# Seven products for two k-tile pairs in the first two down products of both FFNs, with the sums of their rows made behind the last up group

## The chip, the cores and the metric

The kernel runs on one core of one Trainium2 chip. The metric is the device time of one execution in microseconds; the time before is the median of three runs. The engines go by their short names: PE (TensorE, matmuls), PEld (its weight loads), DVE (VectorE), ACT (ScalarE), POOL (GpSimd) and SP (SyncE, which issues the DMAs here).

## The reference

One layer of a streaming encoder on 256 rows of 2048 features, all in fp32:

```python
def swiglu(h, w_gate, w_up, w_down):
    return (jax.nn.silu(h @ w_gate) * (h @ w_up)) @ w_down
...
x = x + 0.5 * swiglu(rms_norm(x, ffn1_norm[l]), ffn1_w_gate[l], ffn1_w_up[l], ffn1_w_down[l])
...
x = x + 0.5 * swiglu(rms_norm(x, ffn2_norm[l]), ffn2_w_gate[l], ffn2_w_up[l], ffn2_w_down[l])
return rms_norm(x, final_norm)
```

Between the two FFNs stand a pooling and gated-linear-attention mixer and a cross attention over 256 memory tokens, which the change does not touch. The FFN's width (D_FF) is 5632: gate and up weights are 2048 x 5632, down weights 5632 x 2048. The profile shows 418 MB read from HBM.

## The kernel before

**Products.** An fp32 value is kept as a high part (rounded to the fp32r form) and a low part (the rest), and a product is three matmuls: high x high, high x low, low x high (`products`). Rows of activations lie transposed in `xs` (the FFN's input) and `ys` (gate times up, or the other blocks' outputs) as 16 k tiles of 128 features by 256 rows, each in two parts. A row half is 128 rows.

**Units.** The stream (`Stream`) cuts all weights into units of 1 MB: two k tiles by 1024 columns in most of the FFN. For each unit SP loads a raw tile (three buffers), ACT copies it into the high part `wh`, DVE subtracts to the low part `wl` (`split_weights`, three buffers each), two units ahead of the matmuls. `in_turn` keeps these copies in the order of the units on each engine. A plain unit is 24 matmuls of 128x128 by 512 columns: two column halves j, two k tiles, two row halves, three matmuls each (`block_t`).

**Seven products.** In a unit whose number in its block is 0, 2 or 4 (`PAIRS`) of the gate and up blocks, the two k tiles and two row halves are taken as a 2 x 2 block matrix, and the unit makes seven products in place of eight (`seven`, 21 matmuls). This needs sums of weight blocks (`add_weights`, tile T on DVE, then a high and low part of T and of three of the raw blocks, xh and xl, in `split_seven`), and sums of row blocks (`part_sums`, made once per FFN and kept in `xe`). The products gather in seven PSUM banks; after the last seven unit `combine` reads four of them (ACT copies one, DVE adds), and at the block's end `join` brings in the rest, once per column half j (`block_s`). The down products of before have no sevens: they are `block_t`, a plain sum in two PSUM tiles.

**PSUM.** Four tiles of two banks, all eight banks. `block_s` holds all four from its first seven unit until `combine`, `block_t` holds two. The turn below takes two for a moment.

**The FFN.** 5632 columns are 11 blocks of 512, worked in parts of 4, 4 and 3 (`FF_PARTS`). The first two parts each are: a gate and an up block of 1024 columns (8 units each), a second gate and up block, then the down product of this part's 16 k tiles (`into_x`): two column halves b of 1024 columns, 8 units each. So a part is 32 units of gate and up and 16 of down; the text calls the four blocks of 8 the first to fourth block of a part. After each up block the product gate x up (`ev_up`) is turned by sixteen transposes on PE in two PSUM tiles `ph` (`turn`), and split into `ys`. The turn of the last up block is queued one unit into the down product. The down product is added to x (`residual`, after `fetch_x` has loaded the columns of x) and written back (`store_x`).

**What sets the order.** `st.op(f, after)` queues a step so many units later; apart from that and from `in_turn`, a scheduler orders each engine's instructions once, at build time, by its own model of their times. On the chip each engine runs its list in that order, and waits where an operand is late. So an instruction that waits holds up everything behind it on its engine. SP's and ACT's and DVE's lists are all made so.

The lines that matter here: L228 and L229 (copy and low part of a weight), L234 and L235 (those of activations), L307 (matmul in `products`), L401 (matmul in `seven`), L363 to L367 (T), L443 to L448 (`combine`), L452 (`join`), L608 (`residual`), L681 (`ev_up`), L691 (transposes of `turn`).

Of the kernel before, what the change touches and what calls it, by code (L numbers as in the profile page):

```python
# [14 lines left out]
P = 128  # L15
# [77 lines left out]
def build(ctx, tc, I, out):  # L93
# [132 lines left out]

    def split_weights(hi, lo, src):
        in_turn("scalar", lambda: nc.scalar.copy(hi, src))  # L228
        in_turn("vector", lambda: nc.vector.tensor_tensor(  # L229
            out=lo, in0=src, in1=f32(hi), op=ALU.subtract  # L230
        ))
# [109 lines left out]
    def part_sums(act, ext, i, g):  # L341

        t = scope["pool"].tile([P, 4 * NB], F32, tag="T", name=uid("T"))
        a = t[:, :NB].rearrange("p (k s) -> p k s", k=2)
        e = t[:, NB : 2 * NB].rearrange("p (n s) -> p n s", n=4)
        nc.vector.tensor_tensor(
            out=a, in0=f32(act[:, 2 * g : 2 * g + 2, 0, :]), in1=f32(act[:, 2 * g : 2 * g + 2, 1, :]),
            op=ALU.add,
        )
        a11, a21, a12, a22 = (a[:, k, h * P : (h + 1) * P] for k in range(2) for h in range(2))  # L350
        nc.vector.tensor_tensor(out=e[:, 3], in0=a11, in1=a21, op=ALU.subtract)
        nc.vector.tensor_tensor(out=e[:, 1], in0=a22, in1=a21, op=ALU.subtract)
        nc.vector.scalar_tensor_tensor(
            out=e[:, 2], in0=e[:, 1], scalar=-1.0, in1=a11, op0=ALU.mult, op1=ALU.subtract
        )
        nc.vector.tensor_tensor(out=e[:, 0], in0=a12, in1=e[:, 2], op=ALU.add)
        split(ext[:, i, 0], ext[:, i, 1], e)
# [27 lines left out]
    def seven(banks, act, ext, i, g, first, later, weights):  # L385
# [3 lines left out]
        n4, n1, s2, s3 = ([ext[:, i, p, n] for p in range(2)] for n in range(4))  # L389
# [6 lines left out]
        order = ("P1", "P7", "P5", "P6", "P2", "P3", "P4") if first else (  # L396
            "P1", "P2", "P3", "P7", "P5", "P6", "P4")
        for n in order:
            (a, b), wh, wl = table[n]
            for j, (x, w) in enumerate(((a, wh), (a, wl), (b, wh))):  # L400
                nc.tensor.matmul(  # L401
                    banks[n], x, w, start=first and j == 0,
                    stop=not later and n in ("P1", "P5", "P6", "P7") and j == 2,
                )

    def block_s(srcs, act, ext, pairs, evict, delays=(0, 0)):

        held, n = {}, len(srcs)

        def open_banks():  # L410
            a, b, c, d = (ptile(uid("pt")) for _ in range(4))
            held["ps"] = (d, c)
            held["parts"] = (a, b)
            held["banks"] = {
                "P1": a[:, 0], "P6": a[:, 1], "P7": b[:, 0], "P5": b[:, 1],
                "P2": c[:, 0], "P4": c[:, 1], "P3": d[:, 0],
            }

        def unit_s(g):
            def fn(weights):  # L420
                if g == pairs[0]:
                    open_banks()
                seven(held["banks"], act, ext, pairs.index(g), g, g == pairs[0], g != pairs[-1],
                      weights)
            return fn

        def unit_p(g):
            def fn(wh, wl):
                wh, wl = (w.rearrange("p (k j n) -> p k j n", j=2, n=NB) for w in (wh, wl))
                for j in (1, 0):  # L430
                    for h in range(2):
                        for kk in range(2):

                            fresh = (j, h) == (0, 1) and g == min(set(range(n)) - set(pairs)) and kk == 0
                            products(held["ps"][j][:, h, :], act, 2 * g + kk, h, wh[:, kk, j],
                                     wl[:, kk, j], fresh, g == n - 1 and kk == 1)
            return fn

        def combine():
# [164 lines left out]
    def residual(scale, b):  # L604

        def evict(j, ps):
# [4 lines left out]
            if j:  # L611
                store_x(b)
        return evict

    def fold(c, gain):
# [10 lines left out]
        for h in range(2):  # L626
            q = tmp.tile([P, NB], F32, tag="j", name=uid("j"), bufs=2)
            nc.scalar.activation(q, x[:, h], AF.Square, accum_out=ss[:, h, c : c + 1])

    def into_x(w, act, scale, gain=None, k0=0, nk=KT, spread_too=True, src=None):  # L630
# [14 lines left out]
    PAIRS = (0, 2, 4)  # L645

    def pair_sums(g, delay):
        def f():
            if g == PAIRS[0]:
                rows["xe"] = scope["pool"].tile(  # L650
                    [P, len(PAIRS), 2, 4, P], F32R, tag="xe", name=uid("xe")
                )
            part_sums(xs, rows["xe"], PAIRS.index(g), g)
        st.op(f, delay)

    class Ext:


        def __getitem__(self, i):
# [650 lines left out]
```

## Time and profile before

| | |
|---|---|
| median of 3 runs | 2132.9 us (2132.69 to 2133.01) |
| the profiled execution | 2133.11 us, span 2131.2 us, mean granted clock 0.999 |
| PE busy | 2111.3 us, 99% of the span, 10032 matmuls and transposes |
| weight loads of PE (PEld) | 1768.5 us, 83% |
| DVE busy | 1427.7 us, 67%, 1189 instructions |
| ACT busy | 1008.0 us, 47%, 890 instructions |
| DMA | 204 GB/s over the span, queue q1 60.5% of 16 engines |

The profile is one execution on the chip. A line such as `L229 DVE TENSOR_TENSOR wl<-T,wh 128x2048 ... x54 | 123.6, 2288 | ...` is a group: its line in the kernel, engine, operation, output and inputs, size, count, busy us in all and mean ns of one, then the idle time of the engine before them and what ended it. A row of waits gives engine and line, what it waited for, us in total, times, and the longest. A row of the chain gives start, us and what ran (`x106`: so many instructions in one piece).

### The profile page before, as it was taken

The numbers are of one execution on the slowest core, as the hardware profiler recorded it, in microseconds if no ns is written. First come the engines' busy times: TensorE is split into PE (matmuls) and PEld (weight loads), VectorE is DVE, ScalarE is ACT, GpSimd is POOL, SyncE is SP. The second block draws the span as 40 slices with busy tenths as digits, with TensorE's granted clock in tenths as the row PEclk, the third lists the DMA queues.
The fourth block names the chain that finished last, engine by engine and source line by source line (L and its number), as shares of the span: only waits on it lengthen the run. The fifth ranks groups of instructions, "written<-read, shape, count | busy, mean of one in ns | idle before, by whom it ended". The sixth has DMA issues, their size and how long they took to land.

```text
span 2131.2 us, 24070 instructions
## 1 busy us (share of the span) xinstructions
PE 2111.3 (99%) x10032; PEld 1768.5 (83%) x10032; DVE 1427.7 (67%) x1189; ACT 1008.0 (47%) x890; POOL 14.2 (1%) x41
## 2 busy tenths in 40 slices
PE   9999999999999999999999999999999999999998
PEld 7878888888888888888888888888888888888886
DVE  8876588856864576565666454567874888658744
ACT  7554354534534545455445443445443455434433
POOL 0000000000000000000000000000000000000001
PEclk9999999999999999999999999999999999999999
DMA  7556665566656655557654555666576665766663
GB/s 277 197 189 234 224 221 195 186 233 226 227 178 234 221 162 180 167 185 278 222 190 161 167 169 171 195 207 207 175 247 217 214 209 175 249 212 223 221 217 119
DMA packets 143316, 435.91 MB, mean 205 GB/s; under 512 B 9828, under 2 KB 13000, under 8 KB 142824
## 3 DMA queue, kind: packets, MB, share of 16 engines
q1 hardware_dynamic: 143176, 434.38, 60.5%
q8 instruction: 78, 1.28, 0.2%
q14 instruction: 30, 0.25, 0.0%
q10 hardware_dynamic: 32, 0.01, 0.0%
HBM read 417.58 MB, written 16.78 MB: 204 GB/s over the span
## 4 chain that ended last, share of the span: by engine, by line
PE 98%; DVE 1%; issue 0%; ACT 0%; DMA 0%; SPq 0%; DVEq 0%; ACTq 0%
PE pt L307 58%; PE pa L292 15%; PE pt L401 12%; PE pb L307 6%; PE pe L307 3%; PE ph L691 1%; PE pl L1084 1%; PE pv L1119 1%; PE px L621 0%; DVE wl L229 0%; ACT wh L228 0%; DMA x<-in_x 0%; PE px L575 0%; PE po L954 0%; PE pa L832 0%
## 5 line engine op out<-in xcount | busy, mean ns | idle before, releaser
L229 DVE TENSOR_TENSOR wl<-raw,wh 128x2048 fp32r<-128x2048 f32 (+2 forms) x328 | 740.2, 2258 | 544.5 <-ACT wh L228 543.9
L228 ACT CAST wh<-raw 128x2048 fp32r<-128x2048 f32 (+2 forms) x328 | 618.5, 1886 | 721.7 <-PE pt L307 490.5
L307 PE MATMUL pt<-wh,xs 128*128 128x512 f32 x1952 | 618.6, 390 | 0.0
L307 PE MATMUL pt<-wh,ys 128*128 128x512 f32 x1728 | 534.7, 389 | 0.0
L307 PEld LDWEIGHTS pt<-wh,xs 128*128 128x128 f32 x1952 | 366.6, 188 | 75.7
L307 PE MATMUL pt<-wl,xs 128*128 128x512 f32 x976 | 380.8, 390 | 0.0
L307 PEld LDWEIGHTS pt<-wh,ys 128*128 128x128 f32 x1728 | 324.1, 188 | 67.0
L307 PE MATMUL pt<-wl,ys 128*128 128x512 f32 x864 | 336.3, 389 | 0.0
L292 PE MATMUL pa<-xs,wh 128*128 128x512 f32 x896 | 317.1, 398 | 2.1 <-DVE t L266 1.7
L292 PE MATMUL pa<-xs,wl 128*128 128x256 f32 x896 | 248.8, 281 | 0.0
L307 PEld LDWEIGHTS pt<-wl,xs 128*128 128x128 f32 x976 | 183.5, 188 | 37.9
L292 PEld LDWEIGHTS pa<-xs,wh 128*128 128x128 f32 x896 | 167.7, 188 | 41.2 <-issue 2.0
L307 PEld LDWEIGHTS pt<-wl,ys 128*128 128x128 f32 x864 | 162.2, 188 | 33.5
L292 PEld LDWEIGHTS pa<-xs,wl 128*128 128x128 f32 x896 | 169.2, 189 | 1.6 <-issue 0.2
L228 ACT CAST wh<-T 128x2048 fp32r<-128x2048 f32 x54 | 103.3, 1912 | 135.6 <-DVE T L367 93.3
L229 DVE TENSOR_TENSOR wl<-T,wh 128x2048 fp32r<-128x2048 f32 x54 | 123.6, 2288 | 65.3 <-ACT wh L228 65.3
L307 PE MATMUL pb<-wh,xs 128*128 128x512 f32 x384 | 121.7, 392 | 0.5 <-DVE ys L211 0.5
L401 PE MATMUL pt<-wh,xe 128*128 128x512 f32 x324 | 108.7, 389 | 0.0
L229 DVE TENSOR_TENSOR xl<-raw,xh 128x1536 fp32r<-128x1536 f32 x54 | 94.5, 1750 | 2.7 <-ACT xh L228 2.7
L228 ACT CAST xh<-raw 128x1536 fp32r<-128x1536 f32 x54 | 79.9, 1479 | 28.9 <-PE pt L401 28.8
L307 PEld LDWEIGHTS pb<-wh,xs 128*128 128x128 f32 x384 | 72.0, 188 | 15.6 <-DVE ys L211 0.7
L401 PE MATMUL pt<-xh,xs 128*128 128x512 f32 x216 | 78.6, 389 | 1.7 <-DVE sg L452 1.7
(203 smaller groups left out, 1666.3 us busy)
## 6 DMA issues: line engine op xcount, KB each, us to landing
raw<-in_ffn_w_down SPq DMA_DIRECT2D x88, 1024.0 KB, 5.5
raw<-in_ffn_w_up SPq DMA_DIRECT2D x80, 1024.0 KB, 5.0
raw<-in_ffn_w_gate SPq DMA_DIRECT2D x77, 1024.0 KB, 5.0
raw<-in_w_in SPq DMA_DIRECT2D x32, 1024.0 KB, 5.2
raw<-in_xattn_w_kv SPq DMA_DIRECT2D x32, 1024.0 KB, 5.2
raw<-in_w_out SPq DMA_DIRECT2D x16, 1024.0 KB, 6.2
raw<-in_xattn_w_q SPq DMA_DIRECT2D x16, 1024.0 KB, 5.2
raw<-in_xattn_w_o SPq DMA_DIRECT2D x16, 1024.0 KB, 5.6
```

The costliest lines, as they stand in the source:

```text
L228: in_turn("scalar", lambda: nc.scalar.copy(hi, src))
L229: in_turn("vector", lambda: nc.vector.tensor_tensor(out=lo, in0=src, in1=f32(hi), op=ALU.subtract))
L292: nc.tensor.matmul(o, w, x, start=k == 0 and i == 0, stop=last and i == 1)
L307: nc.tensor.matmul(ps, a, w, start=first and i == 0, stop=last and i == 2)
L401: nc.tensor.matmul(banks[n], x, w, start=first and j == 0, stop=not later and n in ("P1", "P5", "P6", "P7") and j == 2,)
L691: nc.tensor.transpose(v[:, i, h * P : (h + 1) * P], g[:, h, i * P : (i + 1) * P], ident)
L1084: nc.tensor.matmul(ps[:, t, :M], ys[:, 4 * h + d, a, tok], xa["K"][:, d, b, :], start=i == 0, stop=i == 11,)
L1119: nc.tensor.matmul(ps[:, d, :S], xa["V"][:, m, a, col], xa["PT"][:, m, b, :], start=i == 0, stop=i == 5,)
```

## The change

In the down products of the first two parts of both FFNs, the units of k-tile pairs 0 and 2 (`Y_PAIRS`) become seven units, and the eight pairs of a block are taken in the order 1, 3, 0, 4, 2, 5, 6, 7 (`Y_ORDER`). `block_s` is generalised for this: plain units may come ahead of the first seven unit, the PSUM tiles are opened when first needed, and the eighth bank (P0) takes the plain products. With `merge` given, the block's `combine` is followed right away by two additions of its four sums into x (`early_parts`), and the two joins at the end become plain residual additions; x is written back after column half 0 rather than 1. The sums of rows of `ys` (`y_sums`, tile `ye`) are made during the last up block, four and five units after that block is queued, put behind the latest low part and copy of a weight (`behind_weights`); one of the four sums is written over the row half it replaces in `ys`. The sums of `xs` are made the same way (in a `j` tile rather than in T) and queued 5, 6 and 7 units in, in both FFNs (before: 5, 5, 5 in the first, 3, 4, 5 in the second). The tile `j` has one buffer in place of two.

```diff
--- before.py
+++ after.py
         else:
             latest[engine] = f()
 
+    def behind_weights(f):
+        with tc.issue_after(latest["vector"].ins), tc.issue_after(latest["scalar"].ins):
+            f()
     def split_weights(hi, lo, src):
         in_turn("scalar", lambda: nc.scalar.copy(hi, src))
         in_turn("vector", lambda: nc.vector.tensor_tensor(
     def row_squares(src, c):
 
         for h in range(2):
-            j = tmp.tile([P, S], F32, tag="j", name=uid("j"), bufs=2)
+            j = tmp.tile([P, S], F32, tag="j", name=uid("j"))
             nc.scalar.activation(j, src[h], AF.Square, accum_out=ss[:, h, c : c + 1])
 
     diag, rows = {}, {}
 
 
 
...
+    def jtile():
+        return tmp.tile([P, NB], F32, tag="j", name=uid("j"))
+    class Sums:
+        def __init__(self, name, act, pairs, over):
+            self.name, self.act, self.pairs, self.over = name, act, pairs, over
+        def make(self, g):
+            act, i = self.act, self.pairs.index(g)
+            n = 3 if self.over else 4
+            if i == 0:
+                self.tile = scope["pool"].tile(
+                    [P, len(self.pairs), 2, n, P], F32R, tag=self.name, name=uid(self.name)
+                )
+            a, k = jtile(), slice(2 * g, 2 * g + 2)
+            nc.vector.tensor_tensor(
+                out=a.rearrange("p (k s) -> p k s", k=2), in0=f32(act[:, k, 0, :]),
+                in1=f32(act[:, k, 1, :]), op=ALU.add,
+            )
+            a = a.rearrange("p (n s) -> p n s", n=4)
+            p11, p21, p12, p22 = (a[:, m] for m in range(4))
+            nc.vector.tensor_tensor(out=p11, in0=p11, in1=p21, op=ALU.subtract)
+            nc.vector.tensor_tensor(out=p21, in0=p22, in1=p21, op=ALU.subtract)
+            nc.vector.scalar_tensor_tensor(
+                out=p22, in0=p11, scalar=-1.0, in1=p22, op0=ALU.mult, op1=ALU.subtract
+            )
+            nc.vector.tensor_tensor(out=p12, in0=p12, in1=p22, op=ALU.add)
+            split(self.tile[:, i, 0], self.tile[:, i, 1], a[:, 4 - n :])
+            if self.over:
+                split(act[:, 2 * g, 0, P:], act[:, 2 * g, 1, P:], p11)
+        def parts(self, g):
+            i, n = self.pairs.index(g), 3 if self.over else 4
+            t = [[self.tile[:, i, p, m] for p in range(2)] for m in range(n)]
+            return [[self.act[:, 2 * g, p, P:] for p in range(2)]] + t if self.over else t
 
     def add_weights(u, raw):
         t = scope["pool"].tile([P, 4 * NB], F32, tag="T", name=f"T{u}")
 
         return [parts], None
 
-    def seven(banks, act, ext, i, g, first, later, weights):
+    def seven(banks, act, sums, g, fresh, ends, weights):
         th, tl, rh, rl = weights
         k0, k1, lo, hi = 2 * g, 2 * g + 1, slice(0, P), slice(P, S)
         a11, a12, a22 = ([act[:, k, p, t] for p in range(2)] for k, t in ((k0, lo), (k1, lo), (k1, hi)))
-        n4, n1, s2, s3 = ([ext[:, i, p, n] for p in range(2)] for n in range(4))
+        s3, n1, n4, s2 = sums.parts(g)
         table = {
             "P1": (a11, rh[:, 0], rl[:, 0]), "P3": (n4, rh[:, 1], rl[:, 1]),
             "P2": (a12, rh[:, 2], rl[:, 2]), "P5": (n1, th[:, 0], tl[:, 0]),
             "P7": (s3, th[:, 1], tl[:, 1]), "P6": (s2, th[:, 2], tl[:, 2]),
             "P4": (a22, th[:, 3], tl[:, 3]),
         }
-        order = ("P1", "P7", "P5", "P6", "P2", "P3", "P4") if first else (
+        order = ("P1", "P7", "P5", "P6", "P2", "P3", "P4") if "P1" in fresh else (
             "P1", "P2", "P3", "P7", "P5", "P6", "P4")
         for n in order:
             (a, b), wh, wl = table[n]
             for j, (x, w) in enumerate(((a, wh), (a, wl), (b, wh))):
                 nc.tensor.matmul(
-                    banks[n], x, w, start=first and j == 0,
-                    stop=not later and n in ("P1", "P5", "P6", "P7") and j == 2,
-                )
-
...
+    def block_s(srcs, act, sums, order, evict, merge=None):
+        sevens = [g for g in order if g in sums.pairs]
+        held, seen = {"banks": {}}, set()
+        def banks(*names):
+            t = ptile(uid("pt"))
+            for i, n in enumerate(names):
+                held["banks"][n] = t[:, i]
+            return t
+        def open_whole():
+            if "ps" not in held:
+                c = banks("P2", "P4")
+                held["ps"] = (banks("P3", "P0"), c)
+        def open_parts():
+            held["parts"] = (banks("P1", "P6"), banks("P7", "P5"))
+        names = {(1, 0): "P2", (1, 1): "P4", (0, 0): "P3", (0, 1): "P0"}
 
         def unit_s(g):
             def fn(weights):
...
+                if g == sevens[0]:
+                    open_parts()
+                open_whole()
+                fresh = {f"P{i}" for i in range(1, 8)} - seen
+                seen.update(fresh)
+                ends = ("P1", "P5", "P6", "P7") if g == sevens[-1] else ()
+                seven(held["banks"], act, sums, g, fresh, ends, weights)
             return fn
 
         def unit_p(g):
             def fn(wh, wl):
+                open_whole()
                 wh, wl = (w.rearrange("p (k j n) -> p k j n", j=2, n=NB) for w in (wh, wl))
                 for j in (1, 0):
                     for h in range(2):
+                        n = names[j, h]
                         for kk in range(2):
-
-                            fresh = (j, h) == (0, 1) and g == min(set(range(n)) - set(pairs)) and kk == 0
-                            products(held["ps"][j][:, h, :], act, 2 * g + kk, h, wh[:, kk, j],
-                                     wl[:, kk, j], fresh, g == n - 1 and kk == 1)
+                            products(held["banks"][n], act, 2 * g + kk, h, wh[:, kk, j],
+                                     wl[:, kk, j], n not in seen and kk == 0,
+                                     g == order[-1] and kk == 1)
+                        seen.add(n)
             return fn
 
         def combine():
                 out=e[:, 1:3], in0=b, in1=e[:, 3:4].to_broadcast([P, 2, NB]), op=ALU.add
             )
             nc.vector.tensor_tensor(out=e[:, 3], in0=b[:, 1], in1=e[:, 1], op=ALU.add)
+            if merge is not None:
+                merge(e[:, 2:4], e[:, 0:2])
 
         def join(j):
+            if merge is not None:
+                evict(j, held["ps"][j])
+                return
             e = held["e"][:, 0:2] if j else held["e"][:, 2:4]
             nc.vector.tensor_tensor(
                 out=e, in0=held["ps"][j], in1=e, op=ALU.add if j else ALU.subtract
             )
             evict(j, e)
 
-        for g, src in enumerate(srcs):
-            if g in pairs:
-                st.unit(src, unit_s(g), split_seven, add_weights)
-                if g == pairs[-1]:
+        for g in order:
+            if g in sevens:
+                st.unit(srcs[g], unit_s(g), split_seven, add_weights)
+                if g == sevens[-1]:
                     st.op(combine)
             else:
-                st.unit(src, unit_p(g))
+                st.unit(srcs[g], unit_p(g))
         for j in (1, 0):
-            st.op(lambda j=j: join(j), delays[j])
+            st.op(lambda j=j: join(j))
 
     def block_b(srcs, act, evict, delay=0):
 
         for h in range(2):
             nc.sync.dma_start(X[b][h * P : (h + 1) * P, :], xrows[b][:, h])
 
-    def residual(scale, b):
+    def residual(scale, b, last=1):
 
         def evict(j, ps):
             x = x_cols((2 * b + j) * NB, NB)
             nc.vector.scalar_tensor_tensor(
                 out=x, in0=ps, scalar=scale, in1=x, op0=ALU.mult, op1=ALU.add
             )
-            if j:
+            if j == last:
                 store_x(b)
         return evict
+    def early_parts(scale, b):
+        def merge(minus, plus):
+            for j, e, s in ((1, plus, scale), (0, minus, -scale)):
+                x = x_cols((2 * b + j) * NB, NB)
+                nc.vector.scalar_tensor_tensor(
+                    out=x, in0=e, scalar=s, in1=x, op0=ALU.mult, op1=ALU.add
+                )
+        return merge
 
     def fold(c, gain):
 
...
+    def into_x(w, act, scale, gain=None, k0=0, nk=KT, spread_too=True, src=None,
+               sums=None):
 
         for b in range(2):
             st.op(lambda b=b: fetch_x(b, src), 2)
-            block_t(wwide(w, b * 2 * NB, k0, nk), act, residual(scale, b))
+            cols = wwide(w, b * 2 * NB, k0, nk)
+            if sums is None:
+                block_t(cols, act, residual(scale, b))
+            else:
+                block_s(cols, act, sums, Y_ORDER, residual(scale, b, 0), early_parts(scale, b))
             if gain is not None:
                 for j in range(2):
                     st.op(lambda c=2 * b + j: fold(c, gain), 1)
 
     FF_PARTS = ((0, 4), (4, 4), (8, 3))
 
-    PAIRS = (0, 2, 4)
-
...
+    PAIRS, Y_PAIRS = (0, 2, 4), (0, 2)
+    Y_ORDER = (1, 3, 0, 4, 2, 5, 6, 7)
+    CLEAR = PAIRS[-1] + 2
 
     def ffn(wg, wu, wd, down):
         gate = {}
+        x_sums = Sums("xe", xs, PAIRS, False)
+        y_sums = Sums("ye", ys, Y_PAIRS, True)
 
         def hidden():
             e = scope["pool"].tile([P, 4, NB], F32, tag="sg", name=uid("sg"), bufs=2)
                     )
             split(ys[:, k : k + 4, 0, :], ys[:, k : k + 4, 1, :], v)
 
+        for i, g in enumerate(PAIRS):
+            st.op(lambda g=g: x_sums.make(g), 5 + i)
         for lo, n in FF_PARTS:
+            whole = n == KT // 4
             for b in range(0, n - 1, 2):
                 n0 = (lo + b) * NB
                 if lo == b == 0:
                     block_t(wwide(wg, n0), xs, lambda j, ps: ev_gate(j, ps, 1))
                 else:
-                    block_s(wwide(wg, n0), xs, Ext(), PAIRS, lambda j, c: ev_gate(j, c, 0))
-                block_s(wwide(wu, n0), xs, Ext(), PAIRS, ev_up)
+                    block_s(wwide(wg, n0), xs, x_sums, range(8), lambda j, c: ev_gate(j, c, 0))
+                if whole and b:
+                    for i, g in enumerate(Y_PAIRS):
+                        st.op(lambda g=g: behind_weights(lambda: y_sums.make(g)), CLEAR - 2 + i)
+                block_s(wwide(wu, n0), xs, x_sums, range(8), ev_up)
                 held = {}
                 st.op(lambda held=held: held.update(gate))
-                wait = PAIRS[-1] + 2 if b + 2 < n - 1 else 1
+                wait = CLEAR if b + 2 < n - 1 else 1
                 for j in range(2):
                     st.op(lambda j=j, b=b, held=held: turn(held[j], 4 * (b + j)), wait)
             if n % 2:
...
+            down(wd, 4 * lo, 4 * n, lo + n == FF // NB, y_sums if whole else None)
 
     st.op(lambda: turn_gains(0, G_MIX))
     for c in range(8):
...
-    for g in PAIRS:
-        pair_sums(g, 5)
+    def down_first(wd, k0, nk, last, sums):
+        into_x(wd, ys, 0.5, G_MIX if last else None, k0, nk, src=None if k0 else I["x"][0],
+               sums=sums)
     ffn(I["ffn1_w_gate"][0], I["ffn1_w_up"][0], I["ffn1_w_down"][0], down_first)
     st.op(close_scope, 1)
     st.op(open_scope("s_mix"), 1)
...
```

More of the change, by code (lines that the diff above doesn't have):

```diff
@@ L401, in seven @@
                 nc.tensor.matmul(
[L402 to L417 removed]
+                    banks[n], x, w, start=n in fresh and j == 0, stop=n in ends and j == 2
+                )
+    def block_s(srcs, act, sums, order, evict, merge=None):
[13 more added lines that the diff above has]
+        names = {(1, 0): "P2", (1, 1): "P4", (0, 0): "P3", (0, 1): "P0"}
         def unit_s(g):
             def fn(weights):
[L421 to L424, printed above, removed]
+                if g == sevens[0]:
[5 more added lines that the diff above has]
+                seven(held["banks"], act, sums, g, fresh, ends, weights)
             return fn
```

40 lines of the change are left out of this document (4 added, 36 removed).

## The prediction

> **What bounds the kernel now.** I read the page first (busy shares, the chain that ended last), then what the matmul engine waits for, then the chain and the timelines around a down product and inside a part.
>
> ```profile
> PE 2111.3 (99%) x10032; PEld 1768.5 (83%) x10032; DVE 1427.7 (67%) x1189; ACT 1008.0 (47%) x890; POOL 14.2 (1%) x41
> ...
> PE 98%; DVE 1%; issue 0%; ACT 0%; DMA 0%; SPq 0%; DVEq 0%; ACTq 0%
> ```
>
> PE is the bound: 98% of the chain. A matmul taken off it is time gained, unless PE waits instead. The waits of PE, longest first:
>
> ```profile
> PE pgain L539 <- DMA gain<-in_ffn_norm: 4.1, 1, 4.1
> PE pt L401 <- DVE sg L452: 1.7, 1, 1.7
> PE pa L292 <- DVE t L266: 1.7, 1, 1.7
> PE po L954 <- DVE ST L947: 1.0, 1, 1.0
> ```
>
> All of them make some 10 us of 2131.2. The second is the kind that matters here: a seven-product unit waits because VectorE was at a join. The chain of waits around the second part's first down product, and VectorE's and ScalarE's timelines there:
>
> ```profile
> 421.07 2.04 PE pt L401 x9
> 423.11 24.03 PE pt L307 x106
> 447.14 1.75 PE ph L691 x16
> 448.89 1.15 PE pt L307 x5
> ```
>
> ```profile
> 448.27 1.93 ACT L234 CAST ys<-ph 128x1024 fp32r<-128x1024 f32 x2 [1.68 <-PE ph L691]
> ```
>
> ```profile
> 449.32 2.35 DVE L235 TENSOR_TENSOR ys<-ph,ys 128x1024 fp32r<-128x1024 f32 x2 [0.40 <-ACT ys L234]
> ```
>
> 106 matmuls in 24.03 us are 0.2267 us each. The sixteen transposes (L691) end at 448.89; ScalarE's copies end at 450.20 and VectorE's lows at 451.67, and PE runs straight on, because nothing it does in those 2.8 us reads the turned rows. Load by stretch (the columns after the span are PE, PEld, DVE, ACT, POOL, clock, DMA share, GB/s): the two down halves of the first part, then three of the second part's four gate and up blocks:
>
> ```profile
> 182.00:226.60 44.60, 44.60 (x206) 37.16 (x205) 24.89 (x16) 17.24 (x10) 0.00 (x0) 1.00 0.67 236
> 226.60:271.40 44.80, 44.80 (x199) 37.08 (x199) 28.72 (x19) 18.07 (x10) 0.00 (x0) 1.00 0.61 211
> 271.40:312.40 41.00, 41.00 (x183) 33.95 (x182) 33.95 (x26) 20.15 (x12) 0.00 (x0) 1.00 0.67 231
> 312.40:353.50 41.10, 41.10 (x183) 34.04 (x182) 34.66 (x26) 22.61 (x16) 0.00 (x0) 1.00 0.60 205
> 353.50:397.00 43.50, 43.50 (x202) 36.16 (x201) 37.21 (x30) 22.17 (x15) 0.00 (x0) 1.00 0.58 194
> ```
>
> VectorE has 16 to 20 us free in a down block, 6 to 7 in a block with sevens. So the change spends PE time for VectorE time where there is room, and the question is order, not sum.
>
> **What it removes.** 2 FFNs x 2 parts x 2 column halves x 2 pairs = 16 units go from 24 matmuls to 21: 48 x 0.2267 = 10.88 us off PE. The chain's own pieces agree: 5.44 us for 24 (L307), 4.76 for 21 (L401). DMA is the same: the same weight tiles are loaded. [...]
>
> **What it adds, off PE.** Per seven unit VectorE builds T (1.22 + 0.69 + 0.69) and xl (1.75), ScalarE xh (1.48); per block one combine (ACT 0.59; DVE 0.69 + 1.22 + 0.69) and two merges of 128x1024 at the residual's 1.22. Two sevens, combine and merges make 2 x 4.35 + 2.6 + 2.44 = 13.7 us of VectorE in a down block, against 16 to 20 free: hidden by sum. The row sums (Sums.make over ys) are 0.69, four 128x128 operations of 0.28, a low part of 0.28 and one of about 0.5, so some 2.6 us, twice per part, in the last up block, on top of 32.2 of 41.7 us in that stretch; the copies on ScalarE (47% busy) are short. They stand behind a weight's low part, so the low parts after them come up to 1.4 us later each; the weights are two units ahead there. I cost them at nothing (bounds 0 and 2 x 1.4 per part, 11 in all). Without that cover each microsecond is one of PE. The x sums move from 5, 5, 5 (and 3, 4, 5) to 5, 6, 7 units: three times about 2.5 us of VectorE at each FFN's start, where the weights of the first gate block need no T: nothing. One j buffer for two makes ScalarE's squares wait for each other (0.41 us each), while ScalarE is half idle: nothing. On SP's queue only the order of x loads and stores against weight loads changes; fetch_x of the second half stands behind the merges of the first, 20 us before its use: nothing.
>
> **What it moves, 1: the turn before the down product (four places).** In the new PE order the sixteen transposes come 56 matmuls after the down product starts (37 before), and behind them stand one matmul, then four of pair 4's unit, which read the just-turned rows: first the high parts (ScalarE's copy), at the third matmul the low parts (VectorE's). Then six matmuls open a bank pair that the turn must free. Before, plain units 1 to 3 lay between. From the rows: the first ph's copy can start 0.26 us after its transposes (448.27 against the eighth transpose), takes 1.015, the low part 1.22, and 0.1 to PE: 0.26 + 1.015 + 0.03 + 1.22 + 0.1 = 2.62 us. Cover: 0.65 (the rest of the other ph's transposes) and three matmuls, 0.68. PE waits 1.3 us, at four places 5.2. Bounds: 0.8 if VectorE's low part is not needed at once (ScalarE's copy alone), 2.6 if VectorE is a weight's low part (2.29) late at half the places: 3 to 8 in all.
>
> **What it moves, 2: the join in the second part.** VectorE leaves the second down half with its merges, about 4.5 us later than before (the walk of its queue by the rows above gives the low part of the second part's fourth unit 13.1 us after the part begins; in the trace it is 8.6). The first two blocks have 1.6 to 2.6 us of slack for that. At the third block's start the new VectorE order is: join of the block before, then wl of its first unit, two gate products, wl, the other join, xl, T of the next seven. Before, both T and that wl stood ahead of the first join:
>
> ```profile
> 309.54 2.29 DVE L229 TENSOR_TENSOR wl<-raw,wh 128x2048 fp32r<-128x2048 f32 x1 [0.63 <-ACT wh L228]
> 311.75 0.68 DVE L367 TENSOR_TENSOR T<-T,raw 128x512 f32<-128x512 f32 x1
> 312.35 1.22 DVE L452 TENSOR_TENSOR sg<-pt,sg 128x1024 f32<-128x1024 f32 x1
> 313.49 1.75 DVE L229 TENSOR_TENSOR xl<-raw,xh 128x1536 fp32r<-128x1536 f32 x1
> ```
>
> That timeline is of the second block's start, where T already stands right ahead of the join. With the join first, the first wl ends 0.26 + 1.22 + 2.29 + 0.1 = 3.87 us after PE is half through the last unit; PE wants it after 2.72 + 0.91 = 3.63: a wait of 0.25. T of the third unit then ends near 14.3 us, its copy on ScalarE at 16.2, its low part at 18.5, and PE, which interleaves units 2 and 3 there, asks for copies and low part at about 15.2 and 17.4: waits of 0.9 and 1.1. With 0.35 further on and 1.05 at the last up block's second seven: 3.65 us. In the second FFN the third block has the same order (2.6); the fourth has another one, where I take half of the 1.05. Together 3.65 + 3.1 = 6.75, bounds 0 (each wait is within 1.2 us of none) and 15.75 (below).
>
> **Sum.** -10.88 + 5.2 + 6.75 = +1.1 us on the profiled execution's 2133.11 us, which is 0.2 above the median of 2132.9: 2134.0 us.
>
> **Rivals.** Of the measurement, 0.2% (4.3 us) is about what can be told from no change.
>
> *Only the turn waits (the late copies of the second part vanish).* For: each is about a microsecond, VectorE is 83% busy there, and the turn waits give it time to catch up. Against: the join's place is an order, not a lag. 2132.9 - 10.88 + 5.2 = 2127.2.
>
> *Both are hidden.* For: the kernel before has the same interleaving in the third block with no wait. Against: the transposes' readers follow at once by the order. 2122.0.
>
> *VectorE becomes the bound in the second part (slower).* The wait of 2.25 us at the third block recurs at the second and fourth, in both FFNs: four times more, 9 us: 2134.0 + 9 = 2143. It decides from 2137.2 on, so from 3.2 us of waits beyond my sum: if two of the four come. For: 37.2 of 43.5 us busy even before, and the 1.7 us at the join in the first part. Against: the window still has 6 us.
>
> *PE's clock falls after the new waits.* One unit at half the clock after each turn wait would cost 4 x 5.44 = 21.8 us: 2156. Rows of the profile speak against it (after the span: PE busy and its count, clock, DMA share, GB/s): after the 1.7 us wait at 139 us the granted clock stayed at full:
>
> ```profile
> 139.00:141.00 2.00, 0.30 (x2) 1.00 0.96 381
> 141.00:143.00 2.00, 2.00 (x9) 1.00 0.08 33
> ```
>
> [...]
>
> That the products are not saved is no rival: the program has 48 matmuls fewer.
>
> **How the numbers follow.** Forecast 0.36 (2129 to 2138, its waits bounded as above); turn waits only 0.25; all hidden 0.12; VectorE the bound 0.25; the clock 0.02. Faster 0.25 + 0.12 = 0.37, same 0.36, slower 0.25 + 0.02 = 0.27. The range, 2122 to 2143, leaves out half of the all-hidden case and the upper part of the bound case, some 0.17.
>
> **What would show it.** PE: 48 matmuls fewer, 70 units of 21 for 54. Among PE's waits: four near 1.3 us on ys, by ScalarE or VectorE, right after the turn's transposes (near 195, 452 and twice in the second FFN), each over 0.8; waits on wh, wl or sg at the third block of both second parts, about 1 us each. VectorE's busy time: 16 x 4.35 (T and xl) + 8 x 2.6 (combines) + 8 x 2.44 (merges) + 8 x 2.6 (sums) = 131 us more, so 1558 us or 73% of the span. I am wrong if PE has none of these waits (2122), if only the first kind is there (2127), or if the second kind stands at every block's start of the second parts (2143).

## The result and the profile after

| | before | after |
|---|---|---|
| median | 2133.01 us (2132.63 to 2135.11, 9 runs) | 2138.74 us (2137.09 to 2139.99, 9 runs) |
| ratio | | 1.0022, 95% interval 1.0013 to 1.0031 |
| profiled execution (span) | 2133.11 us (2131.2) | 2139.99 us (2138.2) |
| matmuls and transposes on PE | 10032 | 9984 |
| DVE busy | 1427.7 us | 1541.1 us |

The 48 matmuls are gone, VectorE has 113 us more to do, and the kernel is slower: the saved 10.9 us were spent on waiting, and some 5 us more. The page of the changed kernel, in the two lines that were shown of before (busy time; then the chain that ended last, by engine):

```profile
PE 2109.6 (99%) x9984; PEld 1760.6 (82%) x9984; DVE 1541.1 (72%) x1349; ACT 1040.5 (49%) x930; POOL 15.3 (1%) x41
...
PE 91%; DVE 6%; issue 1%; ACT 1%; DMA 0%; SPq 0%; DVEq 0%; ACTq 0%
```

The busy share of PE hides it (99% in both); the chain shows it: PE carries 91% of it instead of 98%, and VectorE 6%. What PE waits for in the changed kernel (us in total, times, longest; the waits that before has too are left out but for the one at the join, which was 1.7 us once):

```profile
PE pt L312 <- ACT ys L239: 2.8, 4, 0.9
PE pt L429 <- DVE sg L499: 2.5, 3, 1.7
PE pt L429 <- DVE xl L234: 2.1, 2, 1.3
PE pt L312 <- ACT wh L233: 1.7, 2, 0.8
...
PE pt L429 <- ACT wh L233: 1.2, 2, 0.6
```

The first row is the turn, four times, once per down product with sevens. The others are in the second part of each FFN, but for the longest on `sg` (1.7 us), which is before's wait at 139 us in the first part. (Lines have moved: L312 is `products`, L429 `seven`, L499 `join`, L391 to L395 T, L733 `ev_up`, L743 the transposes, L233 and L234 a weight's copy and low part.)

**The turn.** The chain at the second part's first down product, which ran 447.14, 448.89 and straight on before:

```profile
454.86 1.54 PE ph L743 x14
456.40 0.02 issue
456.43 1.02 ACT ys L239
457.45 0.02 issue
457.47 1.24 DVE ys L240
458.71 0.04 issue
458.75 1.65 PE pt L429 x6
```

After the transposes the chain leaves PE, goes through ScalarE's copy and VectorE's low part of the turned rows, and comes back to PE at 458.75, with the six matmuls into a bank pair that the turn had to free. Between the copy's end and those six PE runs the four matmuls of pair 4 that read the new high parts; of the 1.4 us lost here 1.0 is the wait for the copy and the rest the wait for the bank pair.

**The third block of the second part.** First VectorE's timeline at its start, then ScalarE's:

```profile
349.77 1.23 DVE L499 TENSOR_TENSOR sg<-pt,sg 128x1024 f32<-128x1024 f32 x1 [3.24 <-PE pt L312]
350.92 2.28 DVE L234 TENSOR_TENSOR wl<-T,wh 128x2048 fp32r<-128x2048 f32 x1
353.11 1.41 DVE L733 SCALAR_TENSOR_TENSOR sg<-sg,Rcol,sg 128x512 f32<-128x512 f32 x2
354.44 2.29 DVE L234 TENSOR_TENSOR wl<-raw,wh 128x2048 fp32r<-128x2048 f32 x1
356.64 1.22 DVE L499 TENSOR_TENSOR sg<-pt,sg 128x1024 f32<-128x1024 f32 x1
357.77 1.75 DVE L234 TENSOR_TENSOR xl<-raw,xh 128x1536 fp32r<-128x1536 f32 x1
359.44 1.22 DVE L391 TENSOR_TENSOR T<-raw 128x1024 f32<-128x1024 f32 x1
360.57 1.41 DVE L733 SCALAR_TENSOR_TENSOR sg<-sg,Rcol,sg 128x512 f32<-128x512 f32 x2
361.90 0.69 DVE L394 TENSOR_TENSOR T<-T,raw 128x512 f32<-128x512 f32 x1
362.62 0.69 DVE L395 TENSOR_TENSOR T<-T,raw 128x512 f32<-128x512 f32 x1
365.36 2.29 DVE L234 TENSOR_TENSOR wl<-T,wh 128x2048 fp32r<-128x2048 f32 x1 [2.05 <-ACT wh L233]
```

```profile
350.26 1.49 ACT L233 CAST xh<-raw 128x1536 fp32r<-128x1536 f32 x1
363.42 1.91 ACT L233 CAST wh<-T 128x2048 fp32r<-128x2048 f32 x1 [11.68 <-DVE T L395]
```

VectorE in the kernel before at the same place has the last addition of T (L367) ahead of both joins (L452):

```profile
351.02 2.29 DVE L229 TENSOR_TENSOR wl<-raw,wh 128x2048 fp32r<-128x2048 f32 x1 [0.62 <-ACT wh L228]
353.23 0.69 DVE L367 TENSOR_TENSOR T<-T,raw 128x512 f32<-128x512 f32 x1
353.83 1.22 DVE L452 TENSOR_TENSOR sg<-pt,sg 128x1024 f32<-128x1024 f32 x1
```

In the changed kernel VectorE idles 3.24 us waiting for PE to finish the half that the join reads, with T of the next seven unit behind it. ScalarE idles 11.68 us for that T. PE gets copy and low part late. An engine that is 72% busy waits here with work behind it in its own queue.

To compare kernels I use the starts of PE's matmuls in the trace: wherever two stand more than 0.29 us apart, what exceeds 0.227 us counts as lost. By place, in us (turn 1 to 4: the down products of first and second part of the two FFNs; P: the gate and up blocks of the second part):

| kernel | turn 1 | P, FFN 1 | turn 2 | turn 3 | P, FFN 2 | turn 4 |
|---|---|---|---|---|---|---|
| before | 0.1 | 0.2 | 0.1 | 0.1 | 0.2 | 0.1 |
| after | 0.9 | 4.7 | 1.4 | 1.4 | 6.7 | 1.3 |
| only the second parts | 0.1 | 0.2 | 1.4 | 0.1 | 0.2 | 1.4 |
| only the first parts | 0.9 | 4.6 | 0.1 | 1.4 | 4.7 | 0.1 |
| one pair | 0.1 | 4.7 | 0.1 | 0.1 | 4.6 | 0.1 |
| join behind a low part | 0.9 | 3.8 | 1.3 | 1.4 | 3.9 | 1.3 |
| join behind T | 0.9 | 2.3 | 1.3 | 1.4 | 2.3 | 0.5 |
| sevens behind the turn | 0.2 | 5.9 | 1.1 | 1.1 | 4.6 | 1.1 |
| both orders | 0.2 | 2.0 | 0.1 | 1.1 | 2.0 | 0.2 |
| both, joins everywhere | 0.1 | 1.9 | 0.2 | 0.9 | 2.1 | 0.2 |

**The clock.** After's 6.7 in the second FFN holds 1.7 us that are no wait. Rows of three stretches (the columns after the span are PE, PEld, DVE, ACT, POOL, clock, DMA share, GB/s):

```profile
1803.90:1806.90 3.00, 1.29 (x6) 0.43 (x4) 3.00 (x4) 0.10 (x1) 0.00 (x0) 1.00 0.94 302
1806.90:1810.40 3.50, 3.50 (x9) 2.73 (x10) 2.29 (x3) 2.30 (x3) 0.00 (x0) 0.51 0.15 47
912.60:916.10 3.50, 3.50 (x13) 2.97 (x12) 3.40 (x8) 2.08 (x4) 0.00 (x0) 0.51 0.66 262
```

Behind 3 us in which PE worked 1.29 the granted clock fell to about half for some 3.4 us. The same happened in the mixer, at 912.6, where the kernel before's profile shows full clock over the same stretch:

```profile
912.60:916.10 3.50, 3.50 (x23) 3.10 (x22) 3.31 (x8) 2.95 (x5) 0.00 (x0) 1.00 0.41 169
```

The mixer's code is the same in both. From before it to behind it the changed kernel's lag over the old one grows from 1.13 to 2.67 us, so a drop costs about 1.5 us.

The balance of the two profiled executions: -10.9 (matmuls) + 4.6 (turns) + 4.5 + 4.8 (second parts, over before's 0.2, clock taken out) + 1.7 + 1.5 (two drops) = +6.2, of the measured 2138.2 - 2131.2 = 7.0; 0.8 is left over, in spacings under the table's limit; I have not followed it.

### The profile page after: what moved, and what is told of

It is laid out like the page before. It is cut to its first block, busy times and chain, and to the rows that moved or that the text cites. A ratio compares the mean times of both kernels' runs of the same rounds, so it can differ in the third digit from the quotient of the medians.

```text
span 2138.2 us, 24188 instructions
## 1 busy us (share of the span) xinstructions
PE 2109.6 (99%) x9984; PEld 1760.6 (82%) x9984; DVE 1541.1 (72%) x1349; ACT 1040.5 (49%) x930; POOL 15.3 (1%) x41
## 4 chain that ended last, share of the span: by engine, by line
PE 91%; DVE 6%; issue 1%; ACT 1%; DMA 0%; SPq 0%; DVEq 0%; ACTq 0%
PE pt L312 50%; PE pa L297 15%; PE pt L429 14%; PE pb L312 6%; PE pe L312 3%; DVE wl L234 2%; DVE xl L234 1%; ACT wh L233 1%; DVE sg L499 1%; PE pl L1141 1%; PE pv L1176 1%; DVE T L391 1%; PE ph L743 1%; PE px L678 0%; DVE sg L733 0%
## 5 line engine op out<-in xcount | busy, mean ns | idle before, releaser
L234 DVE TENSOR_TENSOR wl<-raw,wh 128x2048 fp32r<-128x2048 f32 (+2 forms) x312 | 703.0, 2256 | 398.5 <-ACT wh L233 397.6
L233 ACT CAST wh<-raw 128x2048 fp32r<-128x2048 f32 (+2 forms) x312 | 587.1, 1884 | 547.0 <-PE pt L312 304.7
L312 PE MATMUL pt<-wh,xs 128*128 128x512 f32 x1952 | 621.7, 391 | 1.7 <-ACT wh L233 1.7
L312 PE MATMUL pt<-wh,ys 128*128 128x512 f32 x1472 | 458.5, 390 | 2.8 <-ACT ys L239 2.8
L312 PEld LDWEIGHTS pt<-wh,xs 128*128 128x128 f32 x1952 | 366.8, 188 | 78.7 <-ACT wh L233 3.2
L312 PE MATMUL pt<-wl,xs 128*128 128x512 f32 x976 | 381.1, 390 | 0.0
L312 PEld LDWEIGHTS pt<-wh,ys 128*128 128x128 f32 x1472 | 276.3, 188 | 60.7 <-ACT ys L239 3.8
L312 PE MATMUL pt<-wl,ys 128*128 128x512 f32 x736 | 286.5, 389 | 0.0
L233 ACT CAST wh<-T 128x2048 fp32r<-128x2048 f32 x70 | 133.9, 1912 | 253.8 <-DVE T L395 226.3
L234 DVE TENSOR_TENSOR wl<-T,wh 128x2048 fp32r<-128x2048 f32 x70 | 160.3, 2290 | 93.9 <-ACT wh L233 93.9
L312 PEld LDWEIGHTS pt<-wl,xs 128*128 128x128 f32 x976 | 183.6, 188 | 38.7 <-DVE wl L234 0.9
L312 PEld LDWEIGHTS pt<-wl,ys 128*128 128x128 f32 x736 | 138.2, 188 | 28.5
L234 DVE TENSOR_TENSOR xl<-raw,xh 128x1536 fp32r<-128x1536 f32 x70 | 122.6, 1751 | 0.0
L312 PE MATMUL pb<-wh,xs 128*128 128x512 f32 x384 | 121.7, 392 | 0.5 <-DVE ys L211 0.5
L233 ACT CAST xh<-raw 128x1536 fp32r<-128x1536 f32 x70 | 103.6, 1480 | 15.3 <-PE pt L429 6.7
L429 PE MATMUL pt<-wh,xe 128*128 128x512 f32 x324 | 109.1, 390 | 1.2 <-ACT wh L233 1.2
L391 DVE TENSOR_TENSOR T<-raw 128x1024 f32<-128x1024 f32 x70 | 85.4, 1220 | 3.7 <-DMA raw<-in_ffn_w_down 2.2
L312 PEld LDWEIGHTS pb<-wh,xs 128*128 128x128 f32 x384 | 72.0, 188 | 15.7 <-DVE ys L211 0.7
```

The costliest lines, as they stand in the source:

```text
L234: in_turn("vector", lambda: nc.vector.tensor_tensor(out=lo, in0=src, in1=f32(hi), op=ALU.subtract))
L312: nc.tensor.matmul(ps, a, w, start=first and i == 0, stop=last and i == 2)
L391: nc.vector.tensor_tensor(out=v[:, 0:2], in0=w[:, 1:3], in1=w[:, 0:1].to_broadcast([P, 2, NB]), op=ALU.add)
L429: nc.tensor.matmul(banks[n], x, w, start=n in fresh and j == 0, stop=n in ends and j == 2)
```

## The experiments

The theory (A): two places lose the time, and each by an order: the reader of the turned rows right behind the turn, and T behind the joins in the second part, which the first part's sevens bring about. The rival (B): VectorE has too much to do from the down products on, wherever the sevens are and in whatever order.

### Half of the change: second parts, first parts

```diff
-            whole = n == KT // 4
+            whole = n == KT // 4 and lo > 0
```

> The sevens only in the down products of the second part of each FFN (the first part's downs as before). Saving by matmul counts: 24 x 0.2267 = 5.44 us. Theory A (the waits come from two places: the turn ahead of the down product, about 1.4 us each, and the join that stands ahead of T in the second part, which only the first part's sevens bring about): the turn waits of the two second parts stay, 2.8 us, none at the second part's third and fourth block; 2133.0 - 5.4 + 2.8 = 2130.4. Theory B (VectorE's added load in the down products as such costs PE time, wherever it is): half of the change's loss, so 2133.0 + 2 to 3 = 2135 to 2136.

```diff
-            whole = n == KT // 4
+            whole = n == KT // 4 and lo == 0
```

> The sevens only in the down products of the first part of each FFN. Saving 5.44 us. Theory A: turn waits 0.9 + 1.4, and all late copies of the second part's third and fourth block, about 4.5 us in each FFN: 2133.0 - 5.4 + 2.3 + 9 = 2138.9, up to 1.7 more for each drop of PE's clock. Theory B (load as such): as the other half, 2135 to 2136.

Measured: only the second parts 2131.77 us (2130.43 to 2132.76, 11 runs), ratio to before 0.9990 (0.9981 to 0.9999); only the first parts 2141.14 us (2139.38 to 2142.17, 5 runs), ratio 1.0034 (1.0021 to 1.0048). Before in the same jobs: 2134.03. The halves are no halves: one gains 2.3 us, the other loses 7.1 us, with the same matmuls saved and the same work added (VectorE 1483.9 and 1484.2 us busy, before 1427.7). That speaks against B as it stands, wherever the sevens are, though what follows the two halves differs: the dense blocks of the second part behind one, the third part behind the other. A had -2.6 and +5.9. PE's waits with the second parts alone, the first two that concern the change:

```profile
PE pt L312 <- ACT ys L239: 1.8, 2, 0.9
PE pt L429 <- DVE sg L499: 1.7, 1, 1.7
```

Two turns, and the join as often as before the change; nothing on `wh` or `xl`. The last up block of the second part holds the sums of rows of `ys` here too, and loses nothing; with the first parts alone it has no such sums and loses 1.8 us. So what it loses does not come from the sums.

### One pair of two

```diff
-    PAIRS, Y_PAIRS = (0, 2, 4), (0, 2)
-    Y_ORDER = (1, 3, 0, 4, 2, 5, 6, 7)
+    PAIRS, Y_PAIRS = (0, 2, 4), (2,)
+    Y_ORDER = (0, 1, 3, 4, 2, 5, 6, 7)
```

> One seven unit per down block in place of two (pair 2 alone; order 0, 1, 3, 4, 2, 5, 6, 7), so three plain units stand ahead and the transposes of the turn have more plain matmuls behind them before pair 4. Saving 24 x 0.2267 = 5.44 us, VectorE's added work about half. Theory A: no turn waits (four vanish), the late copies of the second part stay because the join still stands ahead of T there: 2133.0 - 5.4 + 9 = 2136.6. Theory B: half the load, half the loss, and turn waits gone or halved: 2135 or less, with smaller waits at the third block.

Measured: 2138.08 us (2136.88 to 2138.78, 11 runs), ratio 1.0018 (1.0009 to 1.0027). The turn waits are gone at all four places; the second part loses 4.7 and 4.6 us, about as much as with two pairs (4.7 and, without the clock drop, 5.0), though VectorE has only two thirds of the added work (1501.5 us busy, against 1541.1 with two pairs and 1427.7 before; I had said half). B wanted less. Against before's 2134.03 it is +4.1, A had +3.6.

### The join behind a weight's low part

```diff
-            st.op(lambda j=j: join(j))
+            st.op(lambda j=j: behind_weights(lambda: join(j)) if late and j else join(j))
```

with `late` in the second part's first three gate and up blocks.

> The changed kernel, with the first join of the second part's first three gate and up blocks issued behind the latest low part of a weight on VectorE (and the latest copy on ScalarE), so that it no longer stands ahead of the first unit's low part. Same work, other order. Theory A (order): the 2.3 us at the third block shrink to 1 or less and those at the fourth by half, in both FFNs: 2138.7 - 4 to 6 = 2133 to 2135. Theory B (VectorE's load): the waits move to another place and the time stays at 2138 to 2139.

Measured: 2136.22 us (2134.73 to 2138.72, 11 runs), ratio 1.0012 (1.0003 to 1.0021). By the ratios some 2 us better than the change, short of the 4 to 6 that A expected, and the second parts still lose 3.8 and 3.9. ScalarE at the third block in this kernel:

```profile
362.21 1.91 ACT L233 CAST wh<-T 128x2048 fp32r<-128x2048 f32 x1 [10.37 <-DVE T L395]
```

The first low part now stands ahead of the join, and ScalarE waits 10.37 us for T all the same. By the spacings the third block's loss falls from 2.3 to 1.1 us, and the last up block's rises from 1.8 to 2.2. So the join ahead of the low part is not all of it; the last additions of T still stand behind both joins and the gate products.

### The join behind T

```diff
+    def behind_sums(f):
+        with tc.issue_after(latest["T"].ins):
+            f()
...
-            st.op(lambda j=j: join(j))
+            st.op(lambda j=j: behind_sums(lambda: join(j)) if late and j else join(j))
```

with `latest["T"]` the last addition in `add_weights`, and `late` as above.

> The changed kernel, with the first join of the second part's first three gate and up blocks issued behind the last addition of the latest T on VectorE. That is the kernel before's order there: T of the next seven unit, then the joins. Same work. Theory A2 (what is late is T, and behind it the copy on ScalarE, because the joins and gate products stand ahead of T): the 4.65 us of lost time in the second part of each FFN (sum of matmul spacings beyond the pitch) go to about 1, the turn waits stay: 2138.7 - 7 = 2131 to 2132. Theory B (VectorE has too much to do from the first part's down product on): the waits move, 2136 or more, as when only the first low part was put ahead.

Measured: 2131.53 us (2131.02 to 2134.29, 11 runs), ratio 0.9991 (0.9982 to 1.0000); before in this job and the next three 2134.32. VectorE and ScalarE at the third block:

```profile
351.43 2.28 DVE L238 TENSOR_TENSOR wl<-raw,wh 128x2048 fp32r<-128x2048 f32 x1
353.63 0.68 DVE L399 TENSOR_TENSOR T<-T,raw 128x512 f32<-128x512 f32 x1
354.24 1.22 DVE L503 TENSOR_TENSOR sg<-pt,sg 128x1024 f32<-128x1024 f32 x1
```

```profile
354.43 1.92 ACT L237 CAST wh<-T 128x2048 fp32r<-128x2048 f32 x1 [3.16 <-DVE T L399]
```

T is ready at 354.3 rather than 363.3, and the 3.24 us of idle VectorE ahead of the join are gone. A change of order takes 7.2 us off by the medians, 6.1 by the lowest runs: the same instructions, VectorE as busy (1541.4 us). By the table of the profiles 5.1 us are waits of the second parts and 0.7 the fourth turn, where the scheduler moved other instructions too; 1.7 is the clock drop behind FFN 2's last up block, which this profile does not have. I had expected some 1 us left in each second part. What is left (2.3) stands mainly at the second block's start (0.4) and in the last up block (1.7 and 1.8), whose join was not moved: which order makes that wait is not shown.

### The sevens behind the turn

```diff
-                seven(held["banks"], act, sums, g, fresh, ends, weights)
+                if merge is not None and g == sevens[0]:
+                    with tc.issue_after(latest["turn"].ins):
+                        seven(held["banks"], act, sums, g, fresh, ends, weights)
+                else:
+                    seven(held["banks"], act, sums, g, fresh, ends, weights)
```

with `latest["turn"]` the last transpose of `turn`.

> The changed kernel, with the first seven unit of a down product issued behind the sixteen transposes of the turn on PE, so that 7 to 9 of its matmuls stand between the transposes and pair 4 (1 before). Same work, nothing done on the joins. Turn theory: the wait of 2.62 us less 0.65 is then covered by 1.6 to 2.0 us of matmuls: the four turn waits (0.8, 1.3, 1.3, 1.2, in all 4.6 us) go to 0.5 or less each; the second part stays: 2138.7 - 3 to 4.6 = 2134 to 2136. Rival (the bank pair that the turn must free is what is late, so the wait only moves behind): 2138 or more.

Measured: 2134.76 us (2133.8 to 2137.56, 11 runs), ratio 1.0003 (0.9994 to 1.0012). The chain at the first turn stays on PE:

```profile
193.30 0.98 PE ph L747 x9
194.28 0.46 PE pt L429 x2
194.75 0.76 PE ph L747 x7
195.51 1.60 PE pt L429 x7
197.11 0.91 PE pt L312 x4
198.02 3.40 PE pt L429 x15
```

The first turn's wait is gone: seven of the unit's matmuls stand behind the last transposes. At the other three 1.1 us of 1.3 to 1.4 remain (I had expected 0.5 or less), and there PE's order is 9 transposes, 7 matmuls of the seven unit, 7 transposes, 2 matmuls, then pair 4. So the edit did not bring about there the order that it asked for: most of the cover went in among the transposes, ahead of the copy it was to cover. The kernel with both orders, below, tells the same by its own scheduling: 7, 9 and 8 matmuls behind the transposes at the first, second and fourth turn, and 0.1 to 0.2 us lost; 2 at the third, and 1.1. The time is the expected one (2134 to 2136), but not by the turns alone: it fell by more than their 1.5 us in the table (the lowest runs: 2137.1 and 2133.8). This profile has one clock drop against two; I have not followed the rest. This kernel's 5.9 in the first FFN's second part holds a clock drop, right behind that block's waits:

```profile
363.90:366.90 3.00, 1.63 (x5) 0.84 (x6) 2.52 (x2) 3.00 (x3) 0.00 (x0) 1.00 0.85 325
366.90:370.30 3.40, 3.40 (x9) 2.63 (x10) 3.40 (x3) 0.62 (x1) 0.00 (x0) 0.50 0.18 20
```

### Both orders, and the joins everywhere

The two edits above together; then the same with `late` in all parts' gate and up blocks but the FFN's first gate block and the last up block of the first two parts.

> Both orders: joins of the second part behind T, and the first seven unit of a down product behind the turn. If the two are the whole loss: 2133.0 - 10.9 + 1 to 3 = 2123 to 2125, faster than both kernels. If VectorE's load is the cause underneath: above 2130.

> As the one before, with the join behind T in all parts and all gate and up blocks but the last up block of a part (the first part's 1.9 us at its third block among them, which the kernel before has too). By the order theory 1 to 2 us under the one before, 2121 to 2124; if a join put behind T leaves PE waiting for banks elsewhere, more than the one before.

Measured: both orders 2126.55 us (2126.14 to 2129.04, 6 runs), ratio 0.9967 (0.9955 to 0.9979). That is faster than both kernels: 7.8 us under before's 2134.32 in the same job, 12 under the change. Its remaining waits are almost those of before:

```profile
PE pt L433 <- DVE sg L507: 2.5, 3, 1.7
PE pa L301 <- DVE t L275: 1.7, 1, 1.7
PE po L1020 <- DVE ST L1013: 1.0, 1, 1.0
PE pt L316 <- ACT ys L243: 0.6, 1, 0.6
```

The table's row holds 4.7 us more than before's, so 6.2 of the saved 10.9 us should be left; by the lowest run of each (2132.2 and 2126.1) it is 6.1. I had expected 2123 to 2125, with 1 to 3 us lost; it is not above the 2130 that would have spoken for VectorE's load. With the joins behind T everywhere it is 2130.54 us (2127.81 to 2134.76, 11 runs), ratio 0.9985 (0.9976 to 0.9993): 4 us worse than in the second parts alone, a miss: I had expected 2121 to 2124. Some 1.5 us of that can be a clock drop in the mixer, which this profile has and the other has not; by the lowest runs (2127.8 and 2126.1) it is 1.7 us worse. The first part's wait at the join (1.9 us at 139) did not move, and new lost time appeared in the first part of FFN 2 (1.5 us, 0.3 in the kernel with both orders) and the third parts (0.8 and 0.7, against 0.4 and 0.3). A join put behind T would hold PE's banks longer; that this is the cause, and in which block, is not shown.

## Why the prediction was right or wrong

The time lies in the range (2122 to 2143), 4.7 us above the forecast of 2134.0 and past the bound of 0.2%: it fell on the side to which I gave 0.27. That the range holds it is partly luck: its upper end was set for a rival of which only a part came. Against my sum the joins cost 2.6 us more, the turns 0.6 less, and the profiled execution had two clock drops, 3.2 us, which my sum left out.

- *What it removes*: right. 48 matmuls, 10.9 us; the kernel with both orders shows that the gain is there to be had.
- *The turn, 5.2 us*: right in place, order and size: 0.9, 1.4, 1.4 and 1.3 us less the 0.1 of before, 4.6 us. I had VectorE's low part needed at pair 4's third matmul; in the trace its four matmuls there wait for the copy alone, and the six behind them for the bank pair that the low part frees. That the cover behind the transposes sets the wait was shown by one pair (no waits) and by the sevens behind the turn (the first wait gone).
- *The join in the second part, 6.75 us*: right in mechanism and too small. Third block: 2.25 us predicted, 2.27 in both FFNs; the next wait in it 0.35, measured 0.4. The mis-sized term is the last up block's second seven: 1.05 us predicted in FFN 1, 1.75 measured; half of 1.05 in FFN 2, where I had said that the order was another, and 2.2 measured. So 9.3 us for the two second parts in place of 6.75. For the third block the join behind T shows T's place behind the joins and gate products as the cause (2.27 us to nothing). For the last up block, the term that was too small, the runs show that it comes with the first part's sevens and not with the sums of rows; the cause within it stays open.
- *What I costed at nothing*: the sums of rows, the x sums, one j buffer and the merges. None shows up among PE's waits; in the second parts alone, which hold each of them, the only new waits are the two turns. I made no run on each by itself.
- *VectorE's busy time*: 131 us more predicted, 113 measured. The groups of the page add up as predicted (T of 16 units more at 2.6, xl, eight combines, sixteen merges at 1.218, the sums 21.3: 131); the busy time counts neighbours that overlap once, and 160 more instructions overlap by about 0.1 us each (in the third block's timeline 350.92 + 2.28 is 0.09 past the next start, 353.11).
- *Rival "VectorE becomes the bound"*: the time is past the 3.2 us beyond my sum from which it was to decide, and its pattern came by half: the wait of 2.25 us recurred in the fourth block of the second part of both FFNs (1.75 and 2.2), and not at the second. Its mechanism did not hold at the third block: with two thirds of the load the waits there were as long, and with another order and the full load they were gone. In the second parts as a whole that order removed 5.1 of 9.3 us.
- *Rival "the clock"*: 0.02, at 21.8 us, behind the turns. It was there, in another place and at another price: none behind a turn, one behind the waits of FFN 2's last up block, one in the mixer, 1.5 to 1.7 us each. The row that I held against it (1.7 us of wait at 139 with no drop) holds in all ten profiles, and says nothing of other places. That the clock would stay at half for a whole unit behind each turn wait was my supposition: no run shows it, and in the changed kernel's profile the two drops are 3.41 us each at 0.50, from 912.65 and from 1806.95. The longest wait right ahead of the second is 1.3 us, shorter than the 1.7 us at 139 that no drop followed, so the length of one wait does not tell where a drop comes.

## What to carry to other kernels

An engine with a quarter of its time free (VectorE here, busy for 72%) can still stop the one that bounds the kernel, if an instruction that must wait stands in its queue ahead of one that others need; look at what is queued behind the wait, not at busy shares. When work is moved to such an engine, read the new order of its queue and of its neighbours', and pin the two or three places where a wait shows that producers must stay ahead of joins; pinned everywhere, the time here rose again (2130.54 us against 2126.55). Where a change loses, run it by halves: the half that gained and the half that lost had the same work in them, so two runs told where the loss arises, and one run with nothing but an order changed then told why.

## What the runs showed that I had not expected

The granted clock fell to half for about 3.4 us (0.50 from 912.65 to 916.06 and from 1806.95 to 1810.36 in the changed kernel), once or twice in most of the ten profiled executions, and not only behind long waits: in the mixer around 907 to 914 us in the profiles of the change and of five experiments, not in those of before and of three others. In the 7.6 us ahead of it PE worked 4.94 us in the kernel before too:

```profile
905.00:912.60 7.60, 4.94 (x33) 4.10 (x32) 6.70 (x11) 4.51 (x5) 0.00 (x0) 1.00 0.49 156
```

so the same stretch with the same waits (1.7 and 1.0 us in both) gave a drop in one execution and none in another. In the changed kernel the 3.41 us right ahead of the drop in the mixer (from 909.24) have PE busy for 1.76 us, 52%, and those right ahead of the drop at 1806.95 for 1.71, 50%. The share alone does not decide it: in the kernel before the same stretch of the mixer (3.41 us from 908.11) has the same 1.76 us, and the 3.41 us from 138.0, with the wait at 139 in them, have 1.71 us before and 1.70 in the changed kernel, 50%; the clock stayed at 1.00 behind each of them. What does decide it, these runs do not show.

The times of the kernel before fall in two groups: 2132.3 to 2133.6 us (13 of 27 runs) and 2134.0 to 2135.6 (14) beside the first experiments, 2132.2 to 2133.4 (12 of 28) and 2134.3 to 2135.9 (16) beside the later ones. Their means lie 1.7 and 2.2 us apart, about what one drop costs or a little more. That is also why the median of before is 2133.0 in the first nine runs (two of the upper group) and 2134.0 and 2134.3 later. That the groups are the drops is argued: the mean clock of each run leans that way (0.999 in 9 of the 25 lower runs and in none of the 30 upper ones), but one drop (half the clock for 3.41 us of 2132) is 0.0008 of it, and only profiled executions show where the clock fell.
